# A hand-written order for the RWKV stage of a decoder layer: three units under way, the filling products dealt out in small portions

## The chip, the core and the metric

One core of one Trainium2 chip runs the whole layer. The metric is device time in microseconds (us), the median of several executions. The engines are TensorE (PE, matmul; PEld are its weight loads), VectorE (DVE), ScalarE (ACT), GpSimd (POOL) and SyncE (SP, which here only issues DMAs). ACT and POOL can issue DMAs too.

## What is computed

One decoder layer over 1024 prompt tokens and 8 single-token samples. A normalised input `h` is multiplied with one wide matrix `w_in`, whose columns go to an RWKV-7 branch (8 heads of 64), a sliding-window attention, a cross-attention, and three 1024-wide gates. The branches are projected, multiplied with the sigmoid of their gates, added, projected again, and a feed-forward block follows. The change is in the RWKV branch:

```
for each token t, per head:              # S is 64 x 64
    sa = S @ (-kk_t)
    S  = S * w_t + outer(sa, kk_t * a_t) + outer(v_t, k_t)
    y_t = S @ r_t
y = group_norm(y) * ln_w + ln_b + bonus;  out_a = y * g
```

The kernel takes 64 tokens at a time: inside a chunk the recurrence becomes products of 64 x 64 matrices and the inverse of a unit triangular one, and only S goes from chunk to chunk.

## The kernel before, in words

All products are float32 made of two float32r parts, so each becomes three passes (`hh`/`hl` with `wh`/`wl`, lines 181 to 183). A **piece** is one call of `in_proj` (128 columns of `w_in`): 8 k-steps x 3 passes x 3 token groups of 384, 384 and 264 columns, 72 matmuls. Its weights (512 KB, tile `wst`, line 163) are split by ACT into `wh` (line 173) and by GpSimd into `wl` (line 174, `eng=G`). There are 24 gate pieces (`gates`, evacuated on line 286, stored by SP on line 287), 14 RWKV pieces (`rw_proj`; `pair_proj(j)` makes three of them and stores them to `zs_d`), and 4 for the cross-attention queries (`xhead`).

The RWKV scan is cut into 8 **units** (`unit(jj, q)`: four heads, 256 tokens), Python generators with two `yield`s, so three parts. (1) Loads, decay and key preparation: L456/L457 products, L479 and L496 sums over heads, a small transpose L501, a round trip through DRAM (`bsum`, line 504, back as `rn` and `bv`, line 508), then `BR` and `CK` on DVE (lines 533 to 536). (2) The chunk matrices: products L545, masked by DVE into `GM` (line 548), stored to DRAM (`amat`, line 552) and read back spread out as `AT` (line 574, one buffer); `CK` scaled by `gc` on GpSimd (line 556), transposes L562 and L566; then the **inverse**: 31 steps of two small DVE instructions (lines 581, 583) on tile `X`. (3) `X` goes out (`xmat`, line 585) and comes back into `GM` (line 588); products L597 and L600; the **scan**, four chunks (`cc`), each L616, L619, ACT copy `pt`, L626, ACT copy `UV`, L629, DVE state update (line 631, four per chunk), L633, ACT copy `Y`; then group norm on DVE (lines 651 to 658), transposes L661, gate products L669, and the store of `bv` by SP (line 675).

The order: the loop at the end of the stage advances unit `u + 1` to its first yield, runs unit `u` to its end, advances `u + 1` to its second yield, and traces filling pieces between: pair 2, pair 3, then two gates for each of the next units; one gate, four query heads and one gate around the last unit. What is traced is then ordered by the framework's scheduler, which takes on each engine what its own model finds ready, in the order of tracing where several are. So matmuls of pieces land between those of units. Some edges (`issue_after`, `hold`) keep weight splits from moving too early. Four gate pieces are left for the start of the merge (`gates(24)`); four are made in the cross-attention and four in the sliding-window stage.

Of the kernel before, what the change touches and what calls it, by code (L numbers as in the profile page):

```python
# [89 lines left out]
def tile_step(ctx, tc, I, O):  # L90
    nc = tc.nc
    V, A, G, PE, SY = nc.vector, nc.scalar, nc.gpsimd, nc.tensor, nc.sync
    cnt = [0]

# [181 lines left out]

    gate_d = mk(dr, "gate", [24, P, NT])
    todo = list(range(24))

    def gates(n):  # L280
        for _ in range(min(n, len(todo))):
            i = todo.pop(0)

            def evac(g, s, w, b):
                gt = mk(hp, "gt", [P, w], F32, 2)
                op = A.activation(gt, b, AF.Tanh, scale=0.5)
                SY.dma_start(gate_d[i, :, s:s + w], gt)
                return op
            in_proj(G0 + i * P, evac)
# [35 lines left out]
    hw0 = mk(rk, "hw0", [P, 12])  # L325
    V.tensor_scalar(hw0[:, 0:8], pv[:, C_W0:C_W0 + 8], 0.5, None, op0=ALU.mult)
    V.tensor_scalar(hw0[:, 8:12], pv[:, C_KA:C_KA + 4], -1.0, 1.0, op0=ALU.mult, op1=ALU.add)
    one64 = mk(rk, "one64", [P, CH])
    V.memset(one64, 1.0)
    bvs = mk(cp, "bvs", [P, 4, NS])  # L330
    gs = mk(cp, "gs", [P, 4, NS])
    states = [[mk(rk, f"st{j}{i}", [P, P]) for i in range(2)] for j in range(4)]
    for j in range(4):
        for i in range(2):
            G.memset(states[j][i], 0.0)

    def rw_proj(mt, out):
# [90 lines left out]
    def unit(jj, q):  # L428
# [33 lines left out]
        V.tensor_scalar(aa[:, :n], aa[:, :n], 0.5, 0.5, op0=ALU.mult, op1=ALU.add)  # L462
# [42 lines left out]
        rn, bv = mk(ra, "rn", [P, WS]), mk(rp, "bv", [P, WS], F32, 2)  # L505
        for i, t in enumerate((rn, bv)):
            for hh in range(2):
                SY.dma_start(t[hh * 64:hh * 64 + 64, :n],
                             b_d[u, i, hh].rearrange("i t -> (i t)")[:n].partition_broadcast(64))
        V.tensor_tensor(kk[:, :n], kk[:, :n], rn[:, :n], ALU.mult)  # L510
        V.tensor_tensor(bv[:, :n], bv[:, :n], zv[:, :n], ALU.mult)
        V.tensor_tensor(aa[:, :n], aa[:, :n], kk[:, :n], ALU.mult)
        if end:
            G.tensor_copy(bvs[:, pr], bv[:, W:n].rearrange("p (j n) -> p j n", j=2))
            for i, t in ((0, zr), (2, zk), (3, zv), (4, kk), (5, aa)):
                G.tensor_copy(sv[:, :, i], t[:, W:n].rearrange("p (j n) -> p j n", j=2))
# [17 lines left out]
        V.tensor_tensor(CK[:, :, 0], ch(aa), ch(lw), ALU.mult)  # L534
        V.tensor_tensor(BR[:, :, 1], ch(zr), ex[:, :, 1:CH + 1], ALU.mult)
        V.tensor_tensor(CK[:, :, 1], ch(zk), ch(lw), ALU.mult)
# [3 lines left out]
        for c4 in range(2):  # L540
# [6 lines left out]
            for hh in range(2):  # L547
                V.tensor_tensor(GM[:, 4 * c4:4 * c4 + 4, hh], bb[hh], gmask.unsqueeze(1).to_broadcast([P, 4, P]), ALU.mult)
        gm = GM.rearrange("p c h t -> p (c h) t")
        for k in range(2):  # L550
            ks = slice(32 * k, 32 * k + 32)
            SY.dma_start(a_d[u, :, k].rearrange("m s t -> s m t"), gm[ks, :, ks])

        for x in range(2):
            xs_ = slice(4 * x, 4 * x + 4)
            G.tensor_tensor(CK[:, xs_].rearrange("p c a t -> p c (a t)"), CK[:, xs_].rearrange("p c a t -> p c (a t)"),
                            gc[:, xs_].unsqueeze(2).to_broadcast([P, 4, P]), ALU.mult)
        CKT, UV = mk(rp, "CKT", [P, HN, P], F32, 2), mk(rp, "UV", [P, HN, P], F32, 2)
        for x in range(2):
# [3 lines left out]
            A.activation(CKT[:, 4 * x:4 * x + 4], b, AF.Copy)  # L563
        b = sm_bank([P, 4, P])
        for i in range(4):
            PE.transpose(b[:, i], zv[:, i * P:(i + 1) * P], ident)  # L566
        for par in range(2):
            A.activation(UV[64:128].rearrange("p (c e) v -> p c e v", e=2)[:, :, par], b[par * 64:par * 64 + 64], AF.Copy)

# [3 lines left out]
        AT = mk(ra, "AT", [P, NT])[:, :1024].rearrange("p (s t) -> p s t", t=32)  # L573
        SY.dma_start(AT, a_d[u].rearrange("m k s t -> (m k) s t").unsqueeze(0).to_broadcast([4, 32, 32, 32]))
        X = mk(rp, "X", [P, 8, 32])
        V.tensor_copy(X, xinit)
# [7 lines left out]
        yield  # L584
        SY.dma_start(x_d[u].rearrange("m k (c q) t -> q (m k) c t", q=4), X)
        for k in range(2):
            ks = slice(32 * k, 32 * k + 32)
            SY.dma_start(gm[ks, :, ks], x_d[u, :, k].rearrange("m c t -> c m t"))

        V.transpose(XW[0:32], gm[0:32, :, 0:32])  # L590
        XP = mk(rp, "Y", [32, 16, 32])
        for x in range(2):
# [16 lines left out]
        both = [(e, hh, slice(hh * 64, hh * 64 + 64)) for e in range(2) for hh in range(2)]  # L609
        for cc in range(4):  # L610
            ST = [states[2 * jj + e] for e in range(2)]
            S, S2 = [t[cc % 2] for t in ST], [t[(cc + 1) % 2] for t in ST]
            cs = [cc, 4 + cc]
            pp = cp_bank([P, 2, P])
            for e in range(2):
                PE.matmul(pp[:, e], lhsT=BR[:, cs[e]].rearrange("p a t -> p (a t)"), rhs=S[e], start=e == 0, stop=True,  # L616
# [5 lines left out]
            A.activation(pt, pp[0:64], AF.Copy)  # L622
            pz = cp_bank([P, 512])
# [3 lines left out]
            A.activation(UVc[0:64, :, cc], pu, AF.Copy)  # L627
            for e, hh, hs in both:
                PE.matmul(ps[hs, e], lhsT=CKT[:, cs[e], hs], rhs=UV[:, cs[e], hs], start=True, stop=True)  # L629
            for e, hh, hs in both:  # L630
                V.scalar_tensor_tensor(S2[e][hs, hs], S[e][hs, hs], gc[hs, cs[e]:cs[e] + 1], ps[hs, e], ALU.mult, ALU.add)
# [3 lines left out]
            A.activation(Yc[(cc % 2) * 64:(cc % 2) * 64 + 64, :, cc // 2], pp[64:128], AF.Copy)  # L635
# [1132 lines left out]
```

## Time and profile before

| | |
|---|---|
| median of 3 executions | 2067.08 us (2061.78 to 2068.15) |
| the profiled execution: its time | 2062.78 us |
| its span, first to last instruction | 2061.0 us |
| mean granted TensorE clock | 0.948 |
| RWKV stage, as counted here | 182 to 735 us of the span |

The profile is of one execution; times below are us from the start of its span. PE's busy time is the union of matmul spans, whose ends are modelled and overlap, so a steady stream is read from starts. The granted clock is 1.00 at 2.4 GHz and 0.50 at 1.2 GHz. "Idle before" an instruction names what released it.

### The profile page before, as it was taken

Reading aid. Unit: us, or ns where it says so; the run is one execution under the profiler, and the core shown is the slowest. Engines: PE = TensorE matmul, PEld = TensorE weight load, DVE = VectorE, ACT = ScalarE, POOL = GpSimd, SP = SyncE. Lnnn points to the kernel's source line nnn. Section 1 sums busy time; section 2 is a strip of 40 time slices with the busy share of each in tenths; the row PEclk is TensorE's granted clock in tenths of the full one; section 3 lists DMA queues with packets and bytes.
Section 4 is the critical chain, followed back from the end, with each engine's and each line's share of the span. In section 5 each row is a group of like instructions: output and inputs, shape, how many; then the busy total and the mean of one; then the engine's idle time right before and its main releaser. Section 6 shows DMA issues by size and latency. Waiting matters only on the chain. (4 is left out here: it accounts for less than half of the span.)

```text
span 2061.0 us, 36994 instructions
## 1 busy us (share of the span) xinstructions
PE 1928.9 (94%) x14079; PEld 1834.5 (89%) x14079; DVE 1344.0 (65%) x3247; ACT 755.8 (37%) x1617; POOL 590.7 (29%) x606
## 2 busy tenths in 40 slices
PE   4989999998999989999989999979999998999998
PEld 4879888887888888989979999969999998999997
DVE  7465667576676457477652575687666669788864
ACT  4432323232322335344652123343333344344433
POOL 3422211111111135322020000146655554344421
PEclk9999788799898999999999999989999999999999
DMA  4544322323232145232236346416544448455413
GB/s 142 169 152 130 88 73 80 90 80 93 60 84 70 30 129 168 85 95 79 65 112 212 109 142 206 123 49 197 166 150 137 149 150 288 126 148 159 141 40 101
DMA packets 257104, 250.69 MB, mean 122 GB/s; under 512 B 43102, under 2 KB 204959, under 8 KB 256927
## 3 DMA queue, kind: packets, MB, share of 16 engines
q1 hardware_dynamic: 254656, 241.24, 38.5%
q0 software_dynamic: 2016, 6.53, 1.0%
q8 instruction: 111, 1.82, 0.4%
q14 instruction: 67, 0.54, 0.1%
q10 hardware_dynamic: 254, 0.55, 0.1%
HBM read 174.19 MB, written 74.46 MB: 121 GB/s over the span
## 5 line engine op out<-in xcount | busy, mean ns | idle before, releaser
L181 PE MATMUL mm<-hh,wh 128*128 128x384 f32 (+1 forms) x1152 | 391.7, 340 | 5.7 <-ACT z L342 5.1
L182 PE MATMUL mm<-hl,wh 128*128 128x384 f32 (+1 forms) x1152 | 390.0, 339 | 7.3 <-DVE hl L217 7.3
L183 PE MATMUL mm<-hh,wl 128*128 128x384 f32 (+1 forms) x1152 | 390.5, 339 | 1.3 <-POOL wl L174 1.3
L1555 PE MATMUL z<-h,wl 128*128 128x258 f32 x1488 | 265.6, 287 | 7.9 <-DVE x L1648 4.5
L1555 PE MATMUL z<-h,wh 128*128 128x258 f32 x1488 | 263.2, 285 | 8.1 <-DVE wh L1310 4.9
L182 PEld LDWEIGHTS mm<-hl,wh 128*128 128x128 f32 x1152 | 227.6, 198 | 11.3 <-DVE hl L217 8.2
L181 PEld LDWEIGHTS mm<-hh,wh 128*128 128x128 f32 x1152 | 228.5, 198 | 10.1 <-ACT z L342 5.6
L183 PEld LDWEIGHTS mm<-hh,wl 128*128 128x128 f32 x1152 | 228.3, 198 | 5.1 <-POOL wl L174 1.7
L1555 PEld LDWEIGHTS z<-h,wl 128*128 128x128 f32 x1488 | 217.6, 193 | 9.8 <-ACT wl L1536 5.0
L1555 PEld LDWEIGHTS z<-h,wh 128*128 128x128 f32 x1488 | 216.1, 192 | 9.2 <-DVE wh L1310 5.1
L174 POOL TENSOR_TENSOR wl<-wst,wh 128x1024 fp32r<-128x1024 f32 x48 | 116.9, 2435 | 215.6 <-ACT wh L173 211.1
L1648 DVE TENSOR_TENSOR x<-z,x 128x516 f32<-128x516 f32 x168 | 115.9, 691 | 68.8 <-PE z L1555 65.5
L1555 PE MATMUL z<-l,wl 128*128 128x258 f32 x744 | 154.7, 288 | 3.1 <-DVE l L1310 3.1
L1555 PE MATMUL z<-l,wh 128*128 128x258 f32 x744 | 153.5, 286 | 1.0 <-DVE l L1310 1.0
L173 ACT ACTIVATE wh<-wst 128x1024 fp32r<-128x1024 f32 x84 | 88.8, 1057 | 141.4 <-PE mm L182 75.0
L1555 PEld LDWEIGHTS z<-l,wl 128*128 128x128 f32 x744 | 117.9, 192 | 3.7 <-DVE l L1310 3.6
L1555 PEld LDWEIGHTS z<-l,wh 128*128 128x128 f32 x744 | 117.0, 191 | 1.7 <-DVE l L1310 1.7
L1503 POOL TENSOR_TENSOR sw<-wst 128x256 f32<-128x256 f32 (+1 forms) x56 | 55.1, 984 | 208.0 <-DMA wst<-in_w_down 87.9
L1607 POOL TENSOR_TENSOR us<-us,us 128x516 f32<-128x516 f32 x64 | 96.5, 1519 | 52.0 <-issue 22.1
L1310 DVE TENSOR_TENSOR l<-ub,h 128x516 fp32r<-128x516 f32 (+1 forms) x120 | 92.9, 800 | 6.3 <-ACT h L1335 6.1
L183 PE MATMUL mm<-oh,wl 128*128 128x384 f32 (+1 forms) x288 | 92.2, 320 | 0.0
L182 PE MATMUL mm<-ol,wh 128*128 128x384 f32 (+1 forms) x288 | 92.1, 320 | 0.0
(510 smaller groups left out, 4281.1 us busy)
## 6 DMA issues: line engine op xcount, KB each, us to landing
u<-us SPq DMA_DIRECT2D x112, 258.0 KB
ub<-u SPq DMA_DIRECT2D x112, 258.0 KB
wst<-in_w_in SPq DMA_DIRECT2D x48, 512.0 KB
wst<-in_w_down SPq DMA_DIRECT2D x24, 512.0 KB
gate<-gt SPq DMA_DIRECT2D x48, 192.0 KB
gl<-gate SPq DMA_DIRECT2D x16, 516.0 KB
wst<-in_w_out SPq DMA_DIRECT2D x16, 512.0 KB
wst<-in_w_up SPq DMA_DIRECT2D x16, 512.0 KB
```

Source lines behind the costliest of these rows:

```text
L173: A.activation(hi, st, AF.Copy)
L174: last_lo[:] = [eng.tensor_tensor(lo, st, hi.bitcast(F32), ALU.subtract)]
L181: PE.matmul(out, lhsT=wh, rhs=xh, start=first and k == 0, stop=False)
L182: PE.matmul(out, lhsT=wh, rhs=xl, start=False, stop=False)
L183: end = PE.matmul(out, lhsT=wl, rhs=xh, start=False, stop=last and k == n - 1)
L1310: V.tensor_tensor(lo, x, hi.bitcast(F32), ALU.subtract)
L1503: G.tensor_tensor(s[:, k:k + n], v, w, op)
L1555: op = PE.matmul(z[:, s, :HQ], lhsT=t[:, a, k], rhs=right[ks[k], s, i][b], start=go and k + q == 0, stop=q == 2 and k == nk - 1, skip_grou ...
L1607: G.tensor_tensor(t, x, y, ALU.subtract)
L1648: V.tensor_tensor(c, z, c, ALU.add)
```

## The change

- TensorE and SP get wrappers, `Products` and `Transfers`. While `traced` is true each of their instructions is tied behind the one traced before it on that engine (`keep_in_program_order`). This holds from the first unit to the end of the stage. The other engines stay with the scheduler.
- The pieces become a generator, `filling`, that gives one matmul at a time; `fill(us)` draws matmuls until their cost, 0.45 ns a column, reaches `us`. Its weights are split on DVE (`eng=V`), the next piece's as soon as a piece begins.
- `unit` gets 34 yields. `round_(u)` weaves unit `u` (scan), `u + 1` (inverse, four steps at a time, over the whole round) and `u + 2` (preparation and matrices) with fixed fills. `first` and `matrices` do the same for the two units at the start.
- 13 gates, not 10, follow the pairs in the stage; then one gate, four heads, one gate as before. One gate is left for the merge, not four.
- Off DVE: the group norm's last step, the scaling of `aa`, the copy of `xinit`, half of the state update (its decay, `dS`, is made by ACT ahead of time). The eight short cumulative sums become two long ones with a `carry` mask. Off GpSimd: the weight splits of these pieces and the scaling of `CK`, now eight ACT instructions. The states of two head pairs share a tile.
- Queues: gate stores go from SP to ACT; `oa` and the pieces' `zs` stores go from SP to GpSimd.
- `split_out` of `oa_d` moves from ahead of the first merge branch to its third tile.

```diff
-    V, A, G, PE, SY = nc.vector, nc.scalar, nc.gpsimd, nc.tensor, nc.sync
+    V, A, G = nc.vector, nc.scalar, nc.gpsimd
+    class Products:
+        def kept(self, op):
+            return tc.keep_in_program_order(op) if self.traced else op
...
+    def filling():
+        while pieces:
+            c0, begin = pieces.pop(0)
+            evac, finish = begin()
+            w = pre.pop(c0, None) or wpiece(w_in[:, :, c0:c0 + P], KT, P, eng=V)
+            if pieces and pieces[0][0] not in pre:
+                if not hold and evs[1] is not None:
+                    hold.append((evs[1],))
+                n0 = pieces[0][0]
+                pre[n0] = wpiece(w_in[:, :, n0:n0 + P], KT, P, eng=V)
+            for g, (s, n) in enumerate(GR):
+                b = mm_bank([P, n])
+                for k in range(KT):
+                    for q, (x, y) in enumerate(((0, 0), (0, 1), (1, 0))):
+                        PE.matmul(b, lhsT=w[x][:, k], rhs=h[g][y][:, k], ...)
+                        ... yield n
+                op = evac(g, s, n, b)
+            finish()
+    def fill(us):
+        while us > 0:
+            n = next(filler, None)
+            if n is None:
+                if not pieces:
+                    return
+                filler = filling()
+                continue
+            us -= n * 0.00045
...
-                SY.dma_start(gate_d[i, :, s:s + w], gt)
+            A.dma_start(gate_d[i, :, s:s + w], gt)
...
-        for c in range(HN):
-            cs = slice(c * CH, c * CH + CH)
-            V.tensor_tensor_scan(lw[:, cs], one64, lw[:, cs], 0.0, ALU.mult, ALU.add)
+        for e in range(2):
+            cs = slice(e * Q4, e * Q4 + Q4)
+            V.tensor_tensor_scan(lw[:, cs], carry.rearrange("p c t -> p (c t)"), lw[:, cs], 0.0, ALU.mult, ALU.add)
+        yield
...
-        for x in range(2):
-            xs_ = slice(4 * x, 4 * x + 4)
-            G.tensor_tensor(CK[:, xs_]..., gc[:, xs_]..., ALU.mult)
+        for c in range(HN):
+            A.activation(CK[:, c], CK[:, c], AF.Copy, scale=gc[:, c:c + 1])
...
+            if s % 4 == 3:
+                yield
...
+        def decayed(S, cc):
+            for e, hh, hs in both:
+                A.activation(dS[hs, e], S[hs, e, hs], AF.Copy, scale=gc[hs, 4 * e + cc:4 * e + cc + 1])
...
-                V.scalar_tensor_tensor(S2[e][hs, hs], S[e][hs, hs], gc[...], ps[hs, e], ALU.mult, ALU.add)
+                V.tensor_tensor(S2[hs, :, hs], dS[hs], ps[hs], ALU.add)
...
-            V.tensor_scalar(ys, ys, ag[:, i, 0:1], vv[:, 1, i:i + 1], op0=ALU.subtract, op1=ALU.mult)
+            A.activation(ys, ys, AF.Identity, bias=vv[:, 3, i:i + 1], scale=vv[:, 1, i:i + 1])
...
-        st = SY.dma_start(oa_d[pr, :, t0:t0 + Q4]..., bv[:, 0:W]...)
+        G.dma_start(oa_d[pr, :, t0:t0 + Q4]..., bv[:, 0:W]...)
...
+    def matrices(u):
+        if u < 8:
+            step(u); fill(0.8); step(u); fill(1.6); step(u); fill(0.8); step(u); step(u + 1)
+    def first(u):
+        step(u); fill(2.0); step(u, 2); fill(5.0); step(u); fill(1.5); step(u); fill(5.0); step(u); fill(5.0)
+    def round_(u):
+        a, b = u + 1, u + 2
+        step(u)                       # L597
+        fill(1.6)
+        step(u)                       # L600
+        for cc in range(4):
+            for part in range(3):
+                step(u)
+                if part == 1:
+                    step(a)           # four steps of the inverse
+                if part < 2:
+                    fill(0.65)
+            if cc == 0 and b < 8:
+                step(b)
+            elif cc == 1 and b < 8:
+                step(b); step(b); fill(0.3)
+            else:
+                fill(1.0)
+        step(u)                       # group norm
+        step(a, 2)
+        fill(1.0)
+        step(b)                       # L496
+        fill(1.5)
+        step(b)                       # L501, bsum
+        fill(4.0 if b < 9 else 8.0)
+        step(u)                       # L661, L669, store
+        fill(2.5)
+        step(b)                       # kk to CK
+        step(a, 2)                    # the inverse ends, xmat
+        fill(4.0)
+        matrices(b)
+    for j in (2, 3):
+        pair_pieces(j)
+    gate_pieces(13)
+    PE.traced = SY.traced = True
+    step(0); first(0); matrices(0); step(0, 4); first(1); step(0, 4); matrices(1)
     for u in range(7):
-        next(units[u + 1])
-        if u == 0:
-            FILL[0]()
-        flush(units[u])
-        next(units[u + 1])
-        if u:
-            FILL[u]()
+        round_(u)
+    PE.traced = SY.traced = False
     rwa.close()
...
-    gates(1)
-    heads = [xhead(0)]
-    flush(prev)
-    heads += [xhead(hd) for hd in range(1, 4)]
-    gates(1)
+    gate_pieces(1)
+    for hd in range(4):
+        pieces.append((X0 + hd * P, lambda hd=hd: xparts(hd)))
+    gate_pieces(1)
+    PE.traced = SY.traced = True
+    for u in (6, 7):
+        round_(u)
+    PE.traced = SY.traced = False
+    for _ in filler:
+        pass
```

## Rows read from the trace of the kernel before

**Rows 1.** The page's first part: busy time and share of the span, by engine.

```profile
PE 1928.9 (94%) x14079; PEld 1834.5 (89%) x14079; DVE 1344.0 (65%) x3247; ACT 755.8 (37%) x1617; POOL 590.7 (29%) x606
```

**Rows 2.** Busy time by stretch: length, then PE, PEld, DVE, ACT and POOL busy (instructions), then the granted clock, the DMA share and GB/s. The whole stage, its start, its later stretches, and four gate pieces at the start of the merge.

```profile
182.00:735.00 553.00, 520.85 (x3706) 464.60 (x3705) 356.65 (x1364) 167.32 (x368) 82.65 (x101) 0.89 0.28 78
182.00:300.00 118.00, 105.30 (x652) 96.33 (x652) 79.28 (x244) 32.51 (x67) 20.91 (x31) 0.84 0.31 90
418.00:510.00 92.00, 87.21 (x688) 74.97 (x686) 65.94 (x270) 30.75 (x68) 14.27 (x13) 1.00 0.33 88
510.00:534.00 24.00, 21.41 (x117) 19.04 (x118) 13.48 (x53) 5.13 (x12) 0.25 (x3) 0.50 0.24 67
534.00:626.00 92.00, 87.76 (x702) 77.07 (x700) 61.38 (x255) 29.05 (x68) 16.36 (x17) 1.00 0.30 80
626.00:640.00 14.00, 12.90 (x83) 11.20 (x84) 10.32 (x44) 4.64 (x11) 0.80 (x1) 0.51 0.27 79
1080.00:1118.00 38.00, 38.00 (x246) 38.00 (x245) 6.16 (x5) 11.40 (x17) 4.81 (x2) 1.00 0.82 266
```

**Rows 3.** What PE waited for from 182 to 735 us: total us, times, longest.

```profile
PE sm L496 <- DVE tmp L494: 9.6, 4, 5.1
PE sm L545 <- DVE CK L534: 5.1, 2, 2.8
PE cp L597 <- DMA GM<-xmat: 4.1, 1, 4.1
PE cp L597 <- DVE X L583: 3.6, 1, 3.6
PE sm L545 <- DVE GM L548: 2.5, 4, 0.7
PE cp L661 <- DVE Y L658: 2.0, 1, 2.0
PE sm L545 <- DVE BR L535: 1.9, 2, 1.3
```

**Rows 4.** PE in order of time (start, length): the first matmul of one piece and of the next.

```profile
159.58 0.34 PE L181 MATMUL mm<-hh,wh 128*128 128x384 f32 x1
170.83 0.34 PE L181 MATMUL mm<-hh,wh 128*128 128x384 f32 x1
```

**Rows 5.** One stall in order of time: SP issues `AT`; DVE stands at its first use; PE stands at L496.

```profile
496.75 2.62 SPq L574 DMA_DIRECT2D AT<-amat  x1
510.58 0.19 DVE L581 TENSOR_TENSOR xt<-X,AT 128x31 f32<-128x31 f32 x1 [4.38 <-DMA AT<-amat]
510.77 0.41 DVE L490 TENSOR_SCALAR tmp<-aa,pv,hw 128x256 f32<-128x256 f32 x1
512.59 0.59 PE L496 MATMUL sm<-c_hsel,tmp 128*128 128x2 f32 x2 [5.09 <-DVE tmp L494]
```

**Rows 6.** From L501 to L545 in units 0 and 1, in order of time.

```profile
193.14 0.28 PE L501 MATMUL sm<-c_ident,sn 128*20 128x128 f32 x1
205.95 0.49 PE L545 MATMUL sm<-BR,CK 64*128 64x128 f32 x4 [2.31 <-DVE CK L534]
229.19 0.27 PE L501 MATMUL sm<-c_ident,sn 128*20 128x128 f32 x1 [1.37 <-DVE zso L346]
243.88 0.55 PE L545 MATMUL sm<-BR,CK 64*128 64x128 f32 x2 [2.82 <-DVE CK L534]
```

**Rows 7.** Stretches right after the two waits of rows 6, columns as in rows 2.

```profile
206.40:213.20 6.80, 6.80 (x42) 6.29 (x39) 3.28 (x5) 1.62 (x4) 2.08 (x2) 0.50 0.10 18
244.00:254.20 10.20, 10.20 (x48) 9.09 (x49) 8.06 (x19) 0.62 (x2) 2.61 (x3) 0.50 0.35 108
```

**Rows 8.** A weight split on GpSimd and the DVE instruction that ran beside it.

```profile
358.86 2.47 POOL L174 TENSOR_TENSOR wl<-wst,wh 128x1024 fp32r<-128x1024 f32 x1 [3.15 <-ACT wh L173]
359.01 2.40 DVE L583 TENSOR_TENSOR X<-X,xt 128x64 f32<-128x64 f32 x1
```

**Rows 9.** Groups of instructions (busy us, mean ns | idle before): GpSimd's and DVE's from 182 to 735 us; the last is the split on DVE, 130 to 182 us.

```profile
L174 POOL TENSOR_TENSOR wl<-wst,wh 128x1024 fp32r<-128x1024 f32 x22 | 53.7, 2443 | 146.8 <-ACT wh L173 146.8
L583 DVE TENSOR_TENSOR X<-X,xt 128x60 f32<-128x60 f32 (+24 forms) x248 | 59.5, 240 | 5.7
L631 DVE SCALAR_TENSOR_TENSOR st<-st,gc,cp 64x64 f32<-64x64 f32 x128 | 35.9, 280 | 48.6 <-PE cp L629 30.4 <-ACT UV L627 11.8 <-ACT gt L286 4.1
L658 DVE TENSOR_SCALAR Y<-Y,gag,gvv 128x64 f32<-128x64 f32 x64 | 15.0, 309 | 0.1
L468 DVE TENSOR_TENSOR_SCAN lw<-one,lw 128x64 f32<-128x64 f32 x56 | 12.0, 272 | 0.0
L665 DVE SCALAR_TENSOR_TENSOR bv<-cp,pv,bv 128x256 f32<-128x256 f32 x16 | 7.0, 479 | 3.2 <-PE cp L661 3.1
L174 DVE TENSOR_TENSOR wl<-wst,wh 128x1024 fp32r<-128x1024 f32 x4 | 4.9, 1226 | 4.1 <-ACT wh L173 4.1
```

**Rows 10.** ACT groups, 182 to 735 us, and one DMA issued from ACT's queue at the start.

```profile
L643 ACT ACTIVATE so<-cp 64x128 f32<-64x128 f32 x4 | 1.1, 271 | 1.2 <-PE cp L639 1.2
L465 ACT ACTIVATE sv<-lw 128x16 f32<-128x16 f32 x2 | 0.4, 217 | 4.8 <-DVE lw L461 4.8
1.89 0.26 ACTq L150 DMA_DIRECT2D vrow<-in_rw_w  x1
```

**Rows 11.** The scan of the last unit ends and its group norm follows: PE in order of time.

```profile
687.77 0.63 PE L633 MATMUL cp<-UV,GM 128*64 128x64 f32 x8
697.04 0.33 PE L661 MATMUL cp<-c_ident,Y 128*128 128x128 f32 x1 [1.97 <-DVE Y L658]
```

**Rows 12.** SP issues `xmat` and, once it has landed, the loads back; SP issues weights, and ACT starts on them when they have landed.

```profile
613.21 0.59 SPq L585 DMA_DIRECT2D xmat<-X  x1
618.17 0.85 SPq L588 DMA_DIRECT2D GM<-xmat  x2
1106.91 0.38 SPq L163 DMA_DIRECT2D wst<-in_w_br_c  x1
1110.54 1.06 ACT L173 ACTIVATE wh<-wst 128x1024 fp32r<-128x1024 f32 x1 [1.90 <-DMA wst<-in_w_br_c]
```

**Rows 13.** Stores issued from GpSimd's queue: size, and us from issue to landing.

```profile
xT<-xr POOLq DMA_DIRECT2D x8, 512.0 KB, 9.0
out<-mkn POOLq DMA_DIRECT2D x2, 256.0 KB, 3.4
```

More of the change, by code (lines that the diff above doesn't have):

```diff
@@ L282, in gates, with gate_pieces @@
             i = todo.pop(0)
-            def evac(g, s, w, b):
-                gt = mk(hp, "gt", [P, w], F32, 2)
-                op = A.activation(gt, b, AF.Tanh, scale=0.5)
-                SY.dma_start(gate_d[i, :, s:s + w], gt)
-                return op
-            in_proj(G0 + i * P, evac)
+            in_proj(G0 + i * P, gate_evac(i))
+    def gate_pieces(n):
+        for _ in range(n):
+            i = todo.pop(0)
+            pieces.append((G0 + i * P, lambda i=i: (gate_evac(i), lambda: None)))
     oa_d = mk(dr, "oa", [4, P, NT])
@@ L615, in unit @@
             for e in range(2):
[L616 removed]
+                PE.matmul(pp[:, e], lhsT=BR[:, cs[e]].rearrange("p a t -> p (a t)"), rhs=S[:, e], start=e == 0, stop=True,
                           skip_group_check=e > 0)
@@ L686, in tile_step, with step @@
     units = [unit(jj, q) for jj in range(2) for q in range(4)]
-    FILL = [lambda: pair_proj(2), lambda: pair_proj(3)] + [lambda i=i: gates((2, 2, 2, 2, 2)[i]) for i in range(5)]
-    next(units[0])
-    next(units[0])
-    for u in range(7):
-        next(units[u + 1])
-        if u == 0:
-            FILL[0]()
-        flush(units[u])
-        next(units[u + 1])
-        if u:
-            FILL[u]()
+    def step(u, n=1):
+        if 0 <= u < 8:
+            for _ in range(n):
+                next(units[u], None)
+    def matrices(u):
+        if u < 8:
+            step(u)
+            fill(0.8)
+            step(u)
+            fill(1.6)
+            step(u)
+            fill(0.8)
+            step(u)
+            step(u + 1)
+    def first(u):
+        step(u)
+        fill(2.0)
+        step(u, 2)
+        fill(5.0)
+        step(u)
+        fill(1.5)
+        step(u)
+        fill(5.0)
+        step(u)
+        fill(5.0)
+    def round_(u):
+        a, b = u + 1, u + 2
+        step(u)
+        fill(1.6)
+        step(u)
+        for cc in range(4):
+            for part in range(3):
+                step(u)
+                if part == 1:
[7 more added lines that the diff above has]
+                step(b)
+                fill(0.3)
+            else:
+                fill(1.0)
+        step(u)
+        step(a, 2)
+        fill(1.0)
+        step(b)
+        fill(1.5)
+        step(b)
+        fill(4.0 if b < 9 else 8.0)
+        step(u)
+        fill(2.5)
+        step(b)
+        step(a, 2)
[4 more added lines that the diff above has]
+    gate_pieces(13)
+    pre[pieces[0][0]] = wpiece(w_in[:, :, pieces[0][0]:pieces[0][0] + P], KT, P, eng=V)
+    PE.traced = SY.traced = True
+    step(0)
+    first(0)
+    matrices(0)
+    step(0, 4)
+    first(1)
+    step(0, 4)
+    matrices(1)
+    for u in range(7):
+        round_(u)
+    PE.traced = SY.traced = False
     prev = units[7]
@@ L1267, in tile_step @@
         for m in range(KT):
+            if i == 0 and m == 2:
+                outs.append(split_out(mp, oa_d, 1))
             if i == 1 and m == 4:
```

183 lines of the change are left out of this document (124 added, 59 removed).

## The prediction

> **What bounds the kernel now.** First the page's busy shares [rows 1]: PE is busy 94% of the span, nothing else over 65%. A change that takes no work from PE can win only PE's gaps and PE's slow clock. Next the table by stretch [rows 2]: the RWKV stage, 553 us from 182 to 735, is the place. PE is busy 520.85 us there, but at a granted clock of 0.89; in stretches the clock is 1.00, in others 0.50. Third, PE's waits in the stage [rows 3]: about 32 us, most for DVE.
>
> I split the stage. A piece takes 11.25 us from its first matmul to that of the next one [rows 4]. GpSimd's 22 splits there [rows 9] count 22 pieces: 247.5 us. Waits: 32. Clock: (1 − 0.89) × 553 = 61. What is left, 212.5 us, is the units' own PE work with its switches and short gaps, 26.6 us for each of eight. So 93 us of 553 are loss, and these are what a better order can win.
>
> Where do they come from? A stall in order of time [rows 5]: `AT` is issued at 496.75, DVE stands at its first use until 510.58, idle 4.38 us; behind it on DVE is L490, and PE stands 5.09 us at L496 for that. The clock is 0.50 from 510 to 534 [rows 2]. So one late transfer cost 5 us of wait and then (1 − 0.50) × 24 = 12 us of clock. The start shows it again: from L501 to L545 lie 12.8 us in unit 0 and 14.7 in unit 1, with waits of 2.31 and 2.82 at the end [rows 6], and the clock is 0.50 in the 6.8 and 10.2 us behind them [rows 7]. And GpSimd's split holds up DVE: beside one of 2.47 us an L583 took 2.40 us [rows 8], against a mean of 240 ns [rows 9].
>
> **The change part by part.** *Pieces and merge.* 25 pieces, not 22, run in the stage: + 3 × 11.25 = 33.75 us. The merge starts with three fewer; PE is full there at clock 1.00 [rows 2], so −33.75. But those 38 us also carried 266 GB/s (DMA share 0.82) for the merge, and one gate remains as cover. Weights for the merge took 3.6 us from issue to ACT [rows 12], and splits 1.06 and 1.23 more [rows 12, 9]: 6 us, under the gate's 11. I take +1; bounds 0 and 9 (the share 0.82 × 38 = 31 us of transfers, less 11 of cover, if half must land first). Moving the split of `oa_d` to the third tile takes loads out of that place and is in it.
>
> *DVE.* Off it, for each unit: the state update, 16 of 280 ns [rows 9] become eight, whose size I bound by 0.28 and 0.48 (L665, 256 columns [rows 9]): at 0.35, 1.7 us saved; the norm's last step, 8 × 309 ns, 2.3 after one small new one; scaling of `aa` and `tmp` and the copy of `xinit`, near 1.5; the scans, 8 × 272 ns [rows 9], to two longer ones, between no gain and 1.6, taken as 0.9. 6.4 us by eight, 51. On it: 25 splits of 1226 ns [rows 9], 31. DVE goes from 357 to about 337 us, and loses the lock stalls of [rows 8]. It does not bound, but each instruction in a chain comes sooner.
>
> *ACT.* Each unit gets 16 decays of 64 × 64, between 217 and 271 ns [rows 10], eight `CK` scalings, eight norm steps and a few copies: 9.4 us, 75 for all; 15 gates bring 45 DMA issues of 0.26 [rows 10] to 0.38 [rows 12], 12 to 17. From 167 us to about 255 of 560: hidden by PE, but the decays stand in the scan's chain only if they come late, which `dS` made ahead avoids. In steady rounds that is nothing; without a filler, a hop grows by 0.27.
>
> *Fixed order.* PE now stands wherever the fixed fill is shorter than the chain beside it; SP stands at each DMA that waits, with all later ones behind. So I count covers against chains.
>
> *The two preludes.* `first` and `matrices` deal 18.5 + 3.2 us of fill. L501 to L545 has 5.0 + 5.0 = 10 us under a chain of 12.8 to 14.7 [rows 6]: 3 to 5 us of wait, then 3 to 5 of clock [rows 7]. 8.5 each, 17; bounds 4 and 11 each.
>
> *A steady round.* A round asks 25.3 us of fill, some 26.6 as calls end on whole matmuls, so PE has 26.6 + 26.6 = 53 us. L633 to L661 took 9.3 us [rows 11] and gets fills of 1.0, 1.0, 1.5 and 4.0 and the small products between, 8.9: 0 to 1. L501 to L545 has 4.0 + 2.5 + 4.0 and L661 with its group, 12.1: 1 to 2.5. `AT`, issued after L545, is first used next round: its 10 to 14 us [rows 5] stand against about 10: 0 to 2. L597 should wait for nothing: `xmat`'s 5 us [rows 12] lie under 4.0 + 3.2. With one clock drop of 3.5 us [rows 7] in every other round, 4.7 a round, 28 for six; bounds 2 and 12 a round.
>
> *Where the fill runs out.* 24 × 1032 columns × 0.45 ns = 11.15 us a piece by its own price; 19 pieces give 212. The preludes draw 44 and rounds 0 to 5 160, so 8 are left for round 6, which end inside its third chunk. From there unit 6 has no filler: hops of the last chunk, some 4 us, then L633 to L661, 9.3 [rows 11]: 14 with one hidden microsecond or so. And the next piece has no weights in flight: its load stands on SP behind `xmat` of unit 7 (5.0 us) and takes 3.6 + 1.06 [rows 12]; what of this lies beside the norm I can't see, between 0 and 10, I take 5. In the last two rounds unit 7's norm has 0.65 us of fill against 9.3: 7. Clock afterwards, as [rows 7]: 5. Sum 31; bounds 20 and 45.
>
> *Queues.* `oa` and `zs` go out from GpSimd. Stores from there landed after 3.4 us (256 KB, the size of `oa`) and 9.0 (512 KB) [rows 13]. `bv` has two buffers, so unit u + 2's load of it waits, on SP, until unit u's store has landed. I put it at nothing, as `bv` is not on the way to `CK`; its price otherwise is a rival below.
>
> **Sum.** Loss after: 17 + 28 + 31 = 76, against 93. 33.75 − 33.75 + 1 + 76 − 93 = −16. From the profiled execution's 2062.8 that is 2046.8. It is one of the quicker of those shown; their median, 2067.1, lies 4.3 above. I forecast **2047 us**. About 6 us (0.3%) can be told from no change.
>
> **Rivals.** *The covers hold.* The waits of [rows 3] were an order that the model had wrong, and with DVE free of lock stalls every chain is shorter than those of [rows 6, 11]. Preludes 8, rounds 2 each, 12, the end 16: loss 36, so 2063 + 1 − 57 = 2007. For it: in 418 to 510 and 534 to 626 the clock stood at 1.00 for 92 us each with the old order [rows 2]. Against: the preludes' cover is shorter than the measured chain. 0.22.
>
> *`bv` behind a store (slower).* L669 of unit u is followed by 2.5 us of fill, then SP waits for the slot: 1 us of DVE, 3.4 of store [rows 13], 3.6 for the load (as [rows 12]) and 2.9 for six DVE instructions of 0.48 up to `CK`, if DVE takes the product with `bv` first, as traced: 10.9 against 2.5 + 4.2. L545 waits 4.2 each round; `AT` goes out and comes back 4.2 later, which DVE meets at its head as in [rows 5]; the clock falls, 4. That is 12.4 a round, 74; with 17 and 31 the loss is 122: 2093. It decides at a loss of 92, at 7.3 a round. For it: SP in fixed order can't pass the wait. Against: DVE may be ordered around `bv`. 0.24 for this and what else loses as much.
>
> This rival has a page behind it: the Trainium skill, "SBUF — State Buffer", section "SBUF: two separate sides", warns that GpSimd builds the descriptors of DMAs from its own queue and is locked out by some DVE operations meanwhile, so such DMAs start late; it advises the queues of SP or ACT, the reverse of this change for `oa` and `zs`. By it the landing would exceed [rows 13]; by those rows alone it is 3.4. The page also calls the port that DVE and GpSimd share an exclusive lock, which [rows 8] bear out for splits, 2.40 against 0.24 us.
>
> *The gain is eaten.* Waits move but keep their sum: loss 86 to 98, within 6 us of no change; the dry round alone, at 45 rather than 31, does it: 2061. 0.17, with the case that the order ends near the old one.
>
> **How the numbers follow.** The forecast's own case, loss 55 to 86, gives 2026 to 2057: 0.37. Faster by over 0.3%: 0.37 + 0.22 = 0.59; no change 0.17; slower 0.24. From 1999 to 2091 the range cuts the outer part of the first two rivals, 0.1 on each side at most.
>
> **What would show it.** Right: the stage near 571 us (553 + 34 − 17) at a clock over 0.91; PE without filler ahead of the last L661 but one and at the first piece after it; waits of 3 to 5 us at both first L545; no 2.4 us L583; four gates at the merge become one, PE still full. Wrong: L545 or `AT` waits in every round with the clock at 0.50 behind them (slower rival, with `oa` stores landing late); no gap in round 6 and a clock near 1.00 throughout (2007); a gap ahead of the first merge product over 1 us.

## The result, and the profile after

The changed kernel takes 2097.07 us (median of 4, 2089.48 to 2104.24), the kernel before 2067.61: ratio 1.0148, interval 1.0107 to 1.019. The forecast was 2047, faster; it is slower, and outside the range. The profiled execution is the slowest of the four, 2104.24, and so stands 41.5 us above that of before; some 12 us of this are the two executions' own (7 above the median here, 5 below it before).

All products and all of SP's issues now carry a helper's line (L103, L106, L113), so they are read by their tiles. First the page's busy shares, which answer to [rows 1]:

```profile
PE 1949.4 (93%) x14079; PEld 1847.8 (88%) x14079; DVE 1298.3 (62%) x3070; ACT 849.8 (40%) x1901; POOL 521.6 (25%) x575
```

The table by stretch, columns as in [rows 2]: the stage (now 183 to 797), the one gate left ahead of the merge, and the merge's first products.

```profile
183.00:797.00 614.00, 562.03 (x3928) 501.17 (x3927) 311.84 (x1195) 268.79 (x667) 26.37 (x78) 0.86 0.30 77
1144.50:1155.70 11.20, 11.20 (x74) 10.80 (x73) 3.55 (x4) 4.27 (x8) 0.00 (x0) 1.00 0.76 233
1155.70:1170.00 14.30, 14.30 (x92) 14.30 (x91) 7.98 (x11) 4.65 (x5) 0.00 (x0) 1.00 0.92 328
```

The stage is 61 us longer, not the 18 that were forecast, at a clock of 0.86 against 0.89 [rows 2]. The merge begins without a gap. DVE is down to 312 us, ACT up to 269. PE's waits in the stage, as in [rows 3]:

```profile
PE sm L106 <- ACT Y L782: 11.6, 12, 5.0
PE cp L103 <- DVE st L751: 10.1, 4, 4.0
PE sm L103 <- ACT tmp L569: 9.2, 2, 8.3
PE sm L103 <- DVE GM L645: 4.0, 4, 2.3
PE cp L103 <- DMA GM<-xmat: 3.6, 1, 3.6
PE sm L103 <- ACT lw L555: 3.2, 1, 3.2
```

New against before are long waits inside the scan: for the state update (`st`, L751; before, one of 0.6 us) and for ACT's `lw`. The next table cuts the stage by the forecast's steps. It is worked out from the trace: waits are PE's idle times over 0.25 us; clock is (1 − granted) times the rest of the length; pieces are their matmuls by 11.25/72 us; "own" is what is left, the units' own work. A round begins where TensorE is done with the work ahead of its first L597.

| | length | waits | clock | pieces | own |
|---|---|---|---|---|---|
| before, whole stage | 552.9 | 31.0 | 61.5 | 247.5 | 212.9 |
| after, preludes | 75.3 | 9.4 | 3.0 | 44.8 | 18.1 |
| after, rounds 0 to 5 | 398.6 | 25.5 | 64.3 | 160.9 | 147.9 |
| after, round 6 and last rounds | 140.4 | 15.4 | 8.1 | 75.8 | 41.2 |
| after, whole stage | 614.3 | 50.3 | 75.3 | 281.6 | 207.1 |

Rounds 0 to 5 hold 89.8 of the 125.6 us lost, where the forecast had 28. The scan of rounds 0 to 5, from its first L616 product to its last L633, columns as before: all six rounds after, their sum, and the sum of the same six in the kernel before.

```profile
269.20:301.40 32.20, 31.58 (x204) 25.21 (x204) 17.69 (x80) 14.90 (x39) 0.00 (x0) 0.69 0.29 63
337.10:377.10 40.00, 38.99 (x221) 32.35 (x221) 20.56 (x98) 17.42 (x50) 0.60 (x3) 0.58 0.20 51
411.00:443.70 32.70, 32.33 (x208) 26.84 (x207) 18.35 (x84) 14.97 (x39) 0.00 (x0) 0.69 0.18 49
472.00:508.60 36.60, 32.49 (x211) 27.03 (x209) 18.58 (x85) 15.14 (x39) 0.00 (x0) 0.67 0.25 52
539.50:570.40 30.90, 26.89 (x212) 22.42 (x212) 16.88 (x78) 14.86 (x39) 0.00 (x0) 0.83 0.31 68
599.50:632.40 32.90, 29.05 (x213) 23.81 (x213) 19.49 (x91) 16.90 (x49) 0.61 (x3) 0.84 0.27 70
sum 205.30, PE 191.32 PEld 157.65 DVE 111.56 ACT 94.18 POOL 1.21; mean PE 31.89 PEld 26.28 DVE 18.59 ACT 15.70 POOL 0.20
```

```profile
sum 143.10, PE 140.59 PEld 119.66 DVE 106.28 ACT 50.06 POOL 17.80; mean PE 23.43 PEld 19.94 DVE 17.71 ACT 8.34 POOL 2.97
```

205 us against 143, for nearly the same number of products: this is where the time went. In round 3 one sees how, in order of time: SP issues `AT` and other loads behind it; DVE stands at the first use of `AT` and comes to the state update only then.

```profile
468.25 0.55 SPq L113 DMA_DIRECT2D AT<-amat  x1
468.84 0.48 SPq L113 DMA_DIRECT2D wst<-in_w_in  x1
469.36 3.16 SPq L113 DMA_DIRECT2D zk<-zs  x1
```

```profile
480.55 0.19 DVE L689 TENSOR_TENSOR xt<-X,AT 128x31 f32<-128x31 f32 x1 [7.73 <-DMA AT<-amat]
...
482.23 0.59 DVE L751 TENSOR_TENSOR st<-dS,cp 64x128 f32<-64x128 f32 x2
```

The next chunk's product waited 3.9 us for that update, and the clock is at 0.50 from 480 to 504:

```profile
482.96 1.19 PE L103 MATMUL cp<-st,BR 128*128 128x128 f32 x4 [3.89 <-DVE st L751]
```

```profile
480.10:504.00 23.90, 20.82 (x108) 17.87 (x109) 15.73 (x75) 12.03 (x31) 0.00 (x0) 0.50 0.05 15
```

It is the stall of [rows 5], moved from L496 into the scan. `AT` is issued as the scanned unit begins with L597 (467.9), and so in every round, within 3 us; the kernel before issued it 7 to 21 us ahead.

### The profile page after: what moved, and what is told of

Its sections match the earlier page's. It is cut to its first block, busy times and chain, and to the rows that moved or that the text cites. A ratio compares the mean times of both kernels' runs of the same rounds, so it can differ in the third digit from the quotient of the medians.

```text
span 2102.2 us, 36975 instructions
## 1 busy us (share of the span) xinstructions
PE 1949.4 (93%) x14079; PEld 1847.8 (88%) x14079; DVE 1298.3 (62%) x3070; ACT 849.8 (40%) x1901; POOL 521.6 (25%) x575
## 5 line engine op out<-in xcount | busy, mean ns | idle before, releaser
L103 PE MATMUL mm<-hh,wh 128*128 128x384 f32 (+1 forms) x1152 | 394.3, 342 | 8.3 <-ACT z L417 4.6
L103 PE MATMUL mm<-hl,wh 128*128 128x384 f32 (+1 forms) x1152 | 390.6, 339 | 5.4 <-DVE hl L240 5.4
L103 PE MATMUL mm<-hh,wl 128*128 128x384 f32 (+1 forms) x1152 | 392.7, 341 | 2.2 <-POOL wl L197 1.3
L103 PE MATMUL z<-h,wl 128*128 128x258 f32 x1488 | 265.6, 287 | 11.4 <-DVE x L1852 7.2
L103 PE MATMUL z<-h,wh 128*128 128x258 f32 x1488 | 263.7, 286 | 5.5 <-DVE wh L1514 3.6
L103 PEld LDWEIGHTS mm<-hh,wh 128*128 128x128 f32 x1152 | 230.3, 200 | 14.3 <-ACT z L417 5.0
L103 PEld LDWEIGHTS mm<-hl,wh 128*128 128x128 f32 x1152 | 229.9, 200 | 8.8 <-DVE hl L240 6.1
L103 PEld LDWEIGHTS mm<-hh,wl 128*128 128x128 f32 x1152 | 230.0, 200 | 7.4 <-DVE wl L197 1.7
L103 PEld LDWEIGHTS z<-h,wl 128*128 128x128 f32 x1488 | 217.5, 193 | 13.6 <-DVE x L1852 3.2
L103 PEld LDWEIGHTS z<-h,wh 128*128 128x128 f32 x1488 | 216.2, 192 | 6.6 <-DVE wh L1514 3.8
L103 PE MATMUL z<-l,wl 128*128 128x258 f32 x744 | 154.5, 288 | 3.1 <-DVE l L1514 3.1
L103 PE MATMUL z<-l,wh 128*128 128x258 f32 x744 | 153.8, 286 | 1.0 <-DVE l L1514 1.0
L103 PEld LDWEIGHTS z<-l,wl 128*128 128x128 f32 x744 | 117.8, 193 | 3.7 <-DVE l L1514 3.6
L197 DVE TENSOR_TENSOR wl<-wst,wh 128x1024 fp32r<-128x1024 f32 x61 | 74.7, 1224 | 73.0 <-ACT wh L196 72.5
L103 PEld LDWEIGHTS z<-l,wh 128*128 128x128 f32 x744 | 117.5, 192 | 1.7 <-DVE l L1514 1.7
L103 PE MATMUL mm<-oh,wl 128*128 128x384 f32 (+1 forms) x288 | 92.3, 321 | 0.0
L103 PE MATMUL mm<-ol,wh 128*128 128x384 f32 (+1 forms) x288 | 92.2, 320 | 0.0
```

Source lines behind the costliest of these rows:

```text
L103: return self.kept(nc.tensor.matmul(*a, **k))
L197: last_lo[:] = [eng.tensor_tensor(lo, st, hi.bitcast(F32), ALU.subtract)]
```

## The experiments

Four theories, in the order in which they came up. **A**: `AT` at DVE's head. **B**: the fixed order of TensorE (and of SP) as such. **C**, the forecast's: the fill runs out in round 6. **D**: the scan holds too little filling, and the clock falls for that. A fifth, **E**, came later.

**e1_late_inverse**

```diff
-                if part == 1:
+                if part == 1 and cc:
                     step(a)
...
-        step(a, 2)
+        step(a, 3)
         fill(1.0)
```

> The changed kernel, but the inverse of unit u + 1 begins one chunk later in the round: no step of it in the first chunk, three (not two) after the group norm. Theory A (AT at DVE's head): in the changed kernel AT is issued only after the inverse before it has ended, lands 9 to 12 us later, and DVE stands at its first use with the state update behind it, so that the next chunk's first product waits (3.9, 4.0 and 1.8 us seen) and the clock falls to 0.50 for 10 to 24 us. With one chunk (5 to 6 us) more cover these three waits go, and 10 to 20 us of clock and waits: 2077 to 2087, DVE's idle time before its first use of AT falls from 4 to 9 us to under 3. Rival B (the fixed order as such: any chain beside a short fill stalls): the wait only moves, to L597 behind a later xmat: 2092 to 2102.

2098.91 us, nothing gained. But DVE still began on `AT` only 9 to 13 us after its issue, having stood there for 4 to 10 us: only TensorE and SP are tied, and the scheduler took the inverse ahead as early as its model allowed. The test missed what it aimed at; g1 below repeats it.

**e2_fifteen_gates**

```diff
-    gate_pieces(13)
+    gate_pieces(15)
...
-    gate_pieces(1)
     for hd in range(4):
...
-    gate_pieces(1)
```

> The changed kernel with 15 gates ahead of the last round instead of 13, and the two gates around the last four query heads taken away: the same 15 gates in the stage. Theory C (the forecast's: the fill runs out in round 6): the waits of that round, 10.5 us, and some clock behind them go, for 8 to 16 us less: 2081 to 2089. If the dry round is not what costs (A or B): within 5 us of the changed kernel, 2092 to 2102, with the waits moved into the last two rounds, which have 22 us less of filling.

2083.03 us: theory C holds for its size, 14 us (11 by the ratios to before, 1.0148 and 1.0096, whose intervals overlap). In the changed kernel the end of round 6 shows the wait for the norm and the missing weights (PE, round 6); with fifteen gates its waits fall from 10.5 to 3.9 us.

```profile
688.64 0.48 PE L106 MATMUL sm<-c_ident,Y 128*128 128x128 f32 x1 [5.03 <-ACT Y L782]
...
694.78 0.69 PE L103 MATMUL mm<-hh,wh 128*128 128x384 f32 x1 [1.96 <-ACT wh L196]
```

**e3_no_pin, e4_pin_pe_only, e5_pin_sp_only**

```diff
-    PE.traced = SY.traced = True
+    PE.traced = SY.traced = False     # e3; e4: PE.traced = True; e5: SY.traced = True
```

> The changed kernel with neither TensorE nor SyncE tied to the traced order: the framework's scheduler orders them from the new tracing. Rival B (the fixed order as such costs): the time falls to that of the kernel before or below, 2040 to 2070, with waits in the stage near 30 us and not 50. Theory A (AT comes too late wherever PE's order is from): AT still waits for the end of the inverse that holds its one buffer, DVE stands at it as before: 2080 to 2100.

> The changed kernel with TensorE tied to the traced order and SyncE left to the scheduler. If SyncE's order is a part of the loss (the loads of unit 1's keys stand behind AT at the start: 8.3 us of wait before L496's product): 8 to 15 us less, 2082 to 2089. If the loss lies in AT's place among DVE's instructions or in PE's order: 2092 to 2102.

> The changed kernel with SyncE tied to the traced order and TensorE left to the scheduler: the fourth case beside both tied (2097), TensorE alone (2090) and neither (2041). Theory B (TensorE's fixed order is what costs, some 45 to 50 us of the 56 between the first and the last): 2041 to 2055, waits in the stage under 35 us. If the two ties cost only together: 2085 to 2100 is not reached either, but the time is that of neither, within 5 us of 2041.

2041.22 (ratio to before 0.9891, 0.9843 to 0.994), 2089.69 (between its two cases) and 2052.32 us. So theory B: TensorE's tie costs 48 us without SP's and 45 with it, SP's 11 and 7. (The intervals of these ratios are 0.3 to 0.7% to either side, so what differs by less than 10 us is not settled, SP's share among it.) Untied, the changed kernel is faster than the one before. Its stage (183 to 743.5) and its longest waits:

```profile
183.00:743.50 560.50, 533.87 (x3913) 480.58 (x3912) 306.67 (x1192) 266.11 (x662) 25.97 (x77) 0.91 0.29 81
```

```profile
PE cp L103 <- DVE st L751: 9.7, 4, 4.0
PE cp L103 <- DMA GM<-xmat: 6.3, 1, 6.3
PE sm L103 <- DVE GM L645: 3.1, 3, 1.4
```

By the same working its loss is 26 of waits and 46 of clock. The wait for `st` is still there: theory A is not gone with the tie.

**e6_no_pin_pool_splits, e7_no_pin_coarse, e8_no_pin_ten_gates**, each from e3

```diff
-            w = pre.pop(c0, None) or wpiece(..., eng=V)          # e6, at three places
+            w = pre.pop(c0, None) or wpiece(..., eng=G)
...
-    step(0); first(0); matrices(0); ... matrices(1)              # e7
+    step(0, 18)
...
-        round_(u)
+        step(u + 1, 7)
+        if u == 0:
+            dealt(3)                 # whole pieces
+        step(u, 99)
+        step(u + 1, 12 if u == 6 else 11)
+        if u:
+            dealt((3, 3, 3, 3, 2, 2)[u - 1])
...
-    for u in (6, 7):
-        round_(u)
+    dealt(2)
+    step(7, 99)
...
-    gate_pieces(13)                                              # e8
+    gate_pieces(10)
```

> The untied kernel with the weight splits of its pieces back on GpSimd. If the relief of DVE from GpSimd's splits is worth what the forecast made of it (2.40 us for an L583 beside a split, 25 splits): 10 to 25 us more, 2051 to 2066, and 2.4 us instructions on DVE again. If DVE's own 25 splits of 1.23 us take as much as they give: 2036 to 2048.

> The untied kernel traced in the coarse manner of the kernel before: whole parts of units, whole pieces between them (three behind unit 1's first part, then 3, 3, 3, 3, 2, 2), all moved operations kept. If the finely woven tracing is what the scheduler gains from: 2055 to 2075. If the moved operations and the 13 gates carry the gain: 2033 to 2048.

> The untied kernel with 10 gates ahead of the last round, not 13, so four at the merge again. By the forecast (three pieces cost 33.75 us in the one place as in the other, and the losses stay): within 6 us, 2035 to 2047. If the three pieces fill gaps of the stage: 10 to 20 us more, 2051 to 2061, with the stage less than 34 us shorter.

2058.51, 2193.58 and 2055.61 us. Taking the splits off GpSimd is worth 17 us, as forecast in kind: L691, the L583 of before, has a mean of 243 ns with GpSimd's splits, four of its instructions at 2.2 to 2.4 us, and 209 without. Fewer gates cost 14: the stage is 21.9 us shorter, not 34, as three pieces less leave its last scan without filling (its waits in round 6 are 15.7 us, 4.0 in e3). And e7 missed both its ranges: traced as whole pieces, the filling was drawn forward, 42 to 47 us of it in each of rounds 0 to 3, and rounds 4 and 5 had none. The kernel before, traced as whole pieces too, has 21 to 27 us in each of its rounds 0 to 5, so the coarse tracing alone does not do this; what in the changed pieces does was not tried. Two of these, rounds 4 and 5 of e7:

```profile
588.70:668.20 79.50, 37.36 (x253) 30.61 (x253) 33.95 (x136) 25.43 (x70) 1.93 (x6) 0.56 0.13 32
668.20:751.30 83.10, 40.89 (x266) 34.21 (x266) 34.29 (x140) 24.95 (x69) 4.37 (x8) 0.54 0.09 25
```

**g1_inverse_behind_update, g3_no_pin_behind_update**, the one with both ties, the other with none

```diff
+            with ExitStack() as behind:
+                for op in updated if s == 0 else ():     # the last state update traced
+                    behind.enter_context(tc.issue_after(op.ins))
                 V.tensor_tensor(o, X[...], AT[...], ALU.mult)
...
-                if part == 1:
+                if part == 1 and cc > 1:
                     step(a)
...
-        step(a, 2)
+        step(a, 4)
         fill(1.0)
```

> The changed kernel (both tied) with the inverse begun two chunks later, and its first DVE instruction bound behind the state update traced before it (four steps more after the group norm): AT has landed when DVE comes to it. In the run before with a later inverse DVE's order, which the scheduler makes, still had it 12 us behind AT's issue, so that run did not take the wait away; this one does. Theory A (AT at DVE's head starts the scan's waits and its slow clock): waits for the state update from 10 us to under 2, the scan's clock loss of rounds 0 to 5 from 59 to 25 to 35 us, 2060 to 2075. Theory D (the scan is thin: small products with 0.65 us of filling between, and the clock falls there whatever the wait): the clock loss stays over 45, 2082 to 2097.

> The untied kernel (2041) with the inverse begun two chunks later and bound behind the state update. Theory A: the waits for the state update, 9.7 us, and most of the scan's clock loss of 28 us go: 2015 to 2030. Theory D: 2033 to 2046.

2086.23 and 2013.91 us. In the rounds of both DVE never stands at `AT`'s first use. Untied that is worth 27 us, and the kernel beats both others (ratio to before 0.9751, 0.9702 to 0.9799). Its stage, three rounds' scans and their sum over six, and all its waits over 0.25 us:

```profile
183.00:719.00 536.00, 524.80 (x3905) 471.17 (x3905) 305.57 (x1190) 266.17 (x661) 23.52 (x77) 0.95 0.32 84
```

```profile
337.90:359.30 21.40, 20.95 (x202) 17.66 (x200) 11.97 (x45) 11.91 (x32) 1.74 (x4) 1.00 0.24 66
391.20:412.50 21.30, 21.30 (x203) 18.21 (x201) 11.63 (x45) 12.63 (x34) 0.64 (x3) 1.00 0.27 78
444.40:464.90 20.50, 20.50 (x197) 17.41 (x196) 10.30 (x43) 11.12 (x32) 0.33 (x3) 1.00 0.27 78
...
sum 134.60, PE 134.15 PEld 114.07 DVE 69.80 ACT 73.03 POOL 5.02; mean PE 22.36 PEld 19.01 DVE 11.63 ACT 12.17 POOL 0.84
```

```profile
PE cp L103 <- DMA GM<-xmat: 7.0, 2, 5.8
PE sm L103 <- DVE tmp L592: 1.8, 1, 1.8
PE sm L103 <- DVE GM L647: 0.8, 1, 0.8
PE sm L106 <- ACT Y L787: 0.7, 2, 0.4
PE cp L103 <- DVE st L756: 0.5, 1, 0.5
```

The same scan takes 21 us at clock 1.00 here and 33 to 40 at 0.58 to 0.69 in the changed kernel. Tied (g1) the gain is only 11 us, not clear of the intervals, and the six scans lose nearly as much as in the changed kernel, 14.4 us of waits (13.7 there) and 51 of clock (59; in the texts on the runs a scan's clock loss is taken over its whole length, waits included): with DVE free, others stand. In round 3 it is ACT, whose split waits for the weights that SP issued right behind `AT` at 458.22; the scan's copies `Y` and `pt` are behind it and PE waits 6.18 us:

```profile
472.63 1.06 ACT L196 ACTIVATE wh<-wst 128x1024 fp32r<-128x1024 f32 x1 [7.48 <-DMA wst<-in_w_in]
473.71 0.38 ACT L760 ACTIVATE Y<-cp 64x256 f32<-64x256 f32 x1
```

```profile
477.33 1.11 PE L103 MATMUL cp<-pt,GM 64*64 64x64 f32 x8 [6.18 <-ACT pt L744]
```

**g2_scan_fill**, from e2

```diff
-                    fill(0.65)
+                    fill(1.05)
...
-        fill(4.0 if b < 9 else 8.0)
+        fill(3.5 if b < 9 else 8.0)
...
         step(a, 2)
-        fill(4.0)
+        fill(3.0)
```

> The kernel with fifteen gates ahead (both tied, 2083) with 1.05 us of filling, not 0.65, in the eight places inside the scan of a round, and 0.5 and 1.0 us less in two places after it. Theory D: the scan's clock loss, 61 us in rounds 0 to 5, falls to 30 to 40, 2050 to 2068. Theory A: within 6 us of that kernel, 2077 to 2089.

2097.04 us, 14 slower than e2 and outside both ranges. Theory D falls, at least as a cure beside both ties: with 66 us of filling in the six scans instead of 42 their clock loss went only from 61 to 49, and waits appeared where the filling was taken (9.8 us from L661 to L597, 5.9 in e2).

**g4_bv_later**

```diff
-        bv = mk(rp, "bv", [P, WS], F32, 2)
-        spread(1, bv)
...
-        V.tensor_tensor(bv[:, :n], bv[:, :n], zv[:, :n], ALU.mult)
...
             if c4 == 0:
+                bv = mk(rp, "bv", [P, WS], F32, 2)
+                spread(1, bv)
                 yield
+        V.tensor_tensor(bv[:, :n], bv[:, :n], zv[:, :n], ALU.mult)
```

> The changed kernel (both tied) with the load of bv and its product moved behind the first half of the chunk matrices, so that nothing on the way to the matrices stands behind the store of oa that frees bv's buffer. The forecast's slower rival (that store costs 12 us a round): 2030 to 2045. By the trace of the changed kernel, where the load goes 2.6 to 3 us behind the store and the first matrices wait for 4 us in all: 2088 to 2098.

2100.83 us: the forecast's slower rival was not the cause; that its 2093 lay near the result was luck.

**h1_inverse_early_loads, h2_inverse_pin_pe, h3_inverse_pin_sp**, from g1. Theory E: what the scan pays for is the burst of loads behind `AT`.

```diff
         for t, mt in ((zk, 4), (zr, 0), (zv, 8)):     # h1
+            if mt == 8:
+                yield
...
         if u < 8:
+            step(u + 1)
             step(u)
             fill(0.8)
...
-    PE.traced = SY.traced = True
+    PE.traced = True                                  # h2; h3: SY.traced = True
```

> The changed kernel (both tied), the inverse begun two chunks later behind the update (2086), and the loads of zk and zr of the next unit traced ahead of the chunk matrices, not behind AT: in the runs so far whatever SyncE issues right behind AT lands 9 to 14 us later, inside the scan, and ACT or DVE stand for it with the scan's own copies behind them. Theory E (the burst behind AT is what the scan pays for): scan waits of rounds 0 to 5 from 14 us to under 7, its clock loss from 51 to under 35, 2050 to 2070. Theory B (TensorE's tie as such): 2078 to 2092.

> The same later inverse with TensorE tied and SyncE free. Theory E: SyncE is free to issue the loads of the next unit well ahead of AT, as in the untied runs (22 us ahead), so 2020 to 2050, near the untied 2014. Theory B: 2070 to 2085, as TensorE still stands at its heads.

> The same later inverse with SyncE tied and TensorE free. Theory E: the burst stays, scan waits over 8 us in rounds 0 to 5: 2040 to 2065. Theory B: near the untied 2014, 2012 to 2030.

2093.05, 2067.69 and 2071.77 us. Theory E falls for the keys' loads: the scans' waits halved (14.4 to 7.3 us), but L597 of round 0 now waits 9.6, and the scans' clock loss stayed at 53. The eight cases of ties (the kernel before, run beside each of them, took 2064 to 2069):

| | both | PE alone | SP alone | none |
|---|---|---|---|---|
| inverse as changed | 2097 | 2090 | 2052 | 2041 |
| inverse behind the update | 2086 | 2068 | 2072 | 2014 |

With the later inverse each tie alone costs 54 to 58 us, and the second one 14 to 18 more; with the changed order it is nearly all TensorE's. So h2 comes out near theory B, and h3 does not: B had 2012 to 2030 for it, and SP's tie alone costs as much there as TensorE's.

h2 shows one thing more. Its six scans hold no wait over 0.25 us. Three of them, in the same order, run at clock 1.00 in 23 us; the other three fall to 0.50 on the way. Rounds 3, 4 and 5:

```profile
453.50:476.80 23.30, 23.06 (x208) 18.89 (x207) 12.73 (x62) 12.34 (x34) 0.00 (x0) 1.00 0.12 40
507.20:537.80 30.60, 30.60 (x212) 25.62 (x211) 13.27 (x60) 13.17 (x35) 0.00 (x0) 0.72 0.13 42
567.10:599.10 32.00, 32.00 (x213) 26.42 (x211) 14.09 (x66) 13.15 (x39) 0.27 (x2) 0.73 0.18 44
```

In round 5 the clock fell at 576.9, and the last wait over 0.25 us lay 89 us back. So a wait is not needed for the fall, and theory D, the thin scan, is not ruled out as its cause.

## Why the prediction was wrong, step by step

- *What bounds the kernel*, the split of 553 us and "a better order can win": right. g3 wins 54 of the 93 us of loss (10.7 of waits and 28.4 of clock are left).
- *Pieces and merge*: + 34.1 in the stage; the merge takes up its work without a gap. From the stage's end to the end of the span it is 21.2 us less, where −32.75 was forecast. Counted from the first product behind the stage, the fourteen other runs with one gate there have 23 to 37 us less, e1 and g4, tied like the changed kernel, 29: so the forecast's size was right, and most of the missing 11 us seem to be that execution's.
- *DVE*: 357 to 312 us, below the 337 forecast. The cumulative sums saved about what was taken (two of 677 ns a unit for eight of 272), and the relief from GpSimd is in what was not counted: the two inverse groups fell to 209 and 208 ns from 240 [rows 9] and 222.
- *ACT*: 269 us, 14 more than forecast. The bounds from [rows 10] were too low.
- *Preludes*: 12.4 us against 17, though not where forecast: L545 waited 0.5 at most, and unit 1's L496 8.3 for its keys, issued behind `AT`.
- *End*: 23.5 us against 31, at the places counted; the waits are shorter (norm 5.0, weights 2.0, unit 7's norm 3.4), the clock's share is 8.1 against 5. e2 gets 14 us back.
- **The step that failed is "a steady round, 4.7 a round, 28 for six".** It measured 89.8, 15 a round. Its waits, put at some 3 a round, came to 4.2: 0.3 at L661; 0.6 from there to the next L597, which holds L501 to L545; 1.1 at L597 and L600, which were to wait for nothing; and 2.3 inside the scan, where `AT`'s "0 to 2" belongs. `AT`'s cover was taken as about 10 us, but DVE came to it 3 to 7.5 us after its issue and stood there for 4 to 9. The term that failed by most is the clock's: 3.5 us in every other round was put in, and 10.7 in every round came out, 56 of the 64 us in the six scans (59 with the waits' own time). In the changed kernel the waits fall just ahead of or in the scan, which then runs on at 0.50. [rows 5] and the 24 us at 0.50 behind it in [rows 2] had shown that price, and I took the smaller one of [rows 7].
- *Rivals*: the slower one had, by luck, the size (12.4 a round against 15) and the place at DVE's head behind `AT`, and the wrong source. SP does wait for `oa`: the load of `bv` goes 2.7 to 3.2 us behind that store's issue, once 5.1, but nothing that PE needs soon stands there (g4). The Trainium skill's warning of late starts from GpSimd's queue ("SBUF — State Buffer", section "SBUF: two separate sides"), which stood beside that rival, does not show here: the median landing is no longer than in [rows 13]:

```profile
zs<-zso POOLq DMA_DIRECT2D x6, 516.0 KB, 4.0
oa<-bv POOLq DMA_DIRECT2D x8, 256.0 KB, 2.9
```

- *Fixed order*: "PE now stands wherever the fixed fill is shorter than the chain". I checked three chains and left out the scan, whose copies and updates run on engines that are not tied, in an order made apart from TensorE's. So what the runs put in the place of the failed step is TensorE's tie: without it the same tracing takes 45 to 48 us less (e3 to e5).

What stays open: what in TensorE's tie makes the clock fall in scans with hardly a wait (h1, round 4: 1.6 us of wait ahead, 11.9 of clock) or with none (h2). Untying makes it less, and does not end it by itself: the six scans' clock loss is 59 us with both ties, 28 with neither (e3), and 8 only with the later inverse as well (g3). Neither more filling (g2) nor earlier loads (h1) brought that beside the ties.

## What to carry to other kernels

When an order is fixed on one engine, check the chains through every engine that is not fixed: an instruction waiting for a transfer at the head of DVE or ACT holds up whatever short chain is behind it. Give a slow transfer's first use a place behind the chain that runs meanwhile; here the later inverse with that edge was worth 27 us where the scheduler was left free. Weaving the trace finely and leaving the order to the scheduler did better than fixing it. A clock drop is to be priced by the stretch that follows the wait, not by the wait, and here it came without a wait as well.

## What the runs showed of the hardware

- A load issued right behind `AT` landed with it: `zk`, 256 KB, issued at 595.55, released ACT at 606.88, 11.3 us later, half a microsecond after DVE had begun on `AT` (606.4); weights of 512 KB took 3.6 us elsewhere [rows 12].

```profile
595.55 1.43 SPq L113 DMA_DIRECT2D zk<-zs  x2
...
606.88 0.51 ACT L569 ACTIVATE tmp<-zk,pv 128x256 f32<-128x256 f32 x1 [4.18 <-DMA zk<-zs]
```

- ACT's new instructions, all with a scale from a tile, took longer than the rows that bounded them [rows 10]: 342 ns for 64 x 64, 389 for 128 x 128, and 428 for the norm's 128 x 64, which had taken DVE 309 [rows 9]. Groups of the stage:

```profile
L726 ACT ACTIVATE dS<-st,gc 64x64 f32<-64x64 f32 x128 | 41.7, 342 | 11.9 <-DVE st L751 9.8
L782 ACT ACTIVATE Y<-Y,gvv 128x64 f32<-128x64 f32 x64 | 22.1, 428 | 7.5 <-DVE gvv L779 7.4
L663 ACT ACTIVATE CK<-CK,gc 128x128 f32<-128x128 f32 x64 | 20.4, 389 | 13.4 <-PE sm L103 13.3
```
